# Row factors of the third block ahead of the second's, four row loads at later stages, and a fourth buffer in one temporary pool

## The chip, the cores and the metric

The kernel runs on one core of a Trainium2 chip. The metric is the device time of one execution in microseconds (us); three executions of the kernel before took 1470.12, 1470.48 and 1474.75 us, so its median is 1470.48 us.

## The reference

One layer of a decoder trunk for 4096 prompt tokens and 64 sample tokens (8 sequences of 8), 1024 wide:

```python
def _rmsnorm(x, g):
    xf = x.astype(jnp.float32)
    r = lax.rsqrt(jnp.mean(xf * xf, axis=-1, keepdims=True) + RMS_EPS)
    return (xf * r).astype(x.dtype) * g
...
    h = _rmsnorm(x, g_pre)
    z = h @ w_in
    cb, cc, ch, cg, q, k, v, ag, mq, mg = _split_cols(z)
...
    y = jnp.concatenate([out_a, out_b, out_c], axis=-1) @ w_out
    return x + _rmsnorm(y, g_post), new_conv, new_k, new_v
```

`out_a` is a gated short convolution, `out_b` sliding-window attention with a sink logit, `out_c` attention to 256 memory tokens, each times a gate. The outputs are the new activations and the key, value and convolution caches. The change is in the first part: the row factors `r` of the norm, and the projection `z`.

## The kernel before

The projection `h @ w_in` is done in three phases, each for some of the columns of `w_in` and for all 4160 tokens in 8 blocks of 520. TensorE keeps weights and activations as sums of two parts, named `hi` and `lo` (the rounded value, cast by ScalarE, and the rest, subtracted by VectorE at L361), so that a product takes three matmuls for each piece. A block is done by Strassen's scheme in 7 products; only the first two blocks of phase one (`PLAIN_BLOCKS`) are done as 8 plain products each, called stages (0,0) to (1,7) here. `plain_jobs` (L629) and `plain_loads` (L660) are tables by stage: which jobs for VectorE, ScalarE and GpSimd, and which loads, are issued while TensorE does that stage's product. After the projection come the attention and the output projection. TensorE's instruction order doesn't depend on the tables.

**The row factors.** The tokens are read in natural order in 40 groups of 104 rows (`nat`, 416 KB each), numbered `nat0`, `nat1`, ... in the order of their loads; five groups make a block. `row_step` (L269) squares one group on ScalarE with a running sum (L278); after the fifth group GpSimd turns the sums to factors `r` (L284, L285). For blocks 0 and 2 VectorE puts the factors on diagonals (`rows_diag`, L297, tile `mix_s`), and TensorE sums these with a matrix of ones, which leaves the factors broadcast over the partitions (`rows_product`, L306, 4 matmuls). For the other blocks GpSimd writes the 520 factors to memory (`rowd`, L290), and SyncE (SP in the profile) reads them back broadcast to 128 partitions (`rb<-rowd`, L253, 260 KB). `row_queue` issues that read back when a counter (`row_spreads`, 4 for every block) has run down, one step for each stage. Block 1's factors are applied to its already computed `z` (L625); block 2's are applied to its activations (L337), which are first multiplied by the gain of the norm (L328).

**The loads.** All loads of `nat`, `x` (the transposed activations, `in_xt`) and `rb` are issued by SP, one after the other in program order. A load that has to wait for a buffer, or for data that another DMA writes, holds up what is issued after it. `x` of block 2 goes to buffers `x_2B` (two halves) and `place` (two halves, each in two pieces of 344 and 176 KB, L240).

**Phase three.** `finish_parts` (L402) takes a finished `z` (128x520): ScalarE casts it to `zh` (L411), VectorE forms the rest `kl_` (L413), and SP stores both to `qd`. `zh` and `kl_` lie in temporary buffers of two pools, `t2a` and `t2b` of 3 buffers each, which are taken in turn (`temp`, L171); a buffer is free for its next use when the store from it has landed.

VectorE, ScalarE, GpSimd, SP and TensorE all run in program order through the projection (`manual_schedule`).

Of the kernel before, what the change touches and what calls it, by code (L numbers as in the profile page):

```python
# [12 lines left out]
ALU = mybir.AluOpType  # L13
# [7 lines left out]
NS = 64  # L21
# [23 lines left out]
PLAIN_BLOCKS = 2  # L45
# [7 lines left out]
def hybrid_layer(ctx: ExitStack, tc: tile.TileContext, a: dict):  # L53
    nc = tc.nc
    TE, V, S, G, DMA = nc.tensor, nc.vector, nc.scalar, nc.gpsimd, nc.sync
# [7 lines left out]
    ident = const.tile([P, P], F32, name="ident")  # L63
# [6 lines left out]
    diag = const.tile([P, 2 * HW], F32, name="mix_s")  # L70
# [25 lines left out]
    own = ExitStack()  # L96
# [3 lines left out]
    def z_pool(where, name, w=2):  # L100
        return where.enter_context(tc.tile_pool(name=name, bufs=1))

    def open_phase(ph):
        nonlocal tp, natp, pa2, pa1, wide
        wide = 0 if ph == 0 else 2

        if ph == 0:
            z = [z_pool(kept_z, f"z{n}") for n in range(4)]
            natp = own.enter_context(tc.tile_pool(name="nat", bufs=2))
            zp[2] = [*z, z_pool(own, "z4")]  # L110
            kept_z.z4 = zp[2][-1]
        elif ph == 1:
            zp[2].remove(kept_z.z4)
            zp[2][:0] = [z_pool(own, f"z{n}") for n in (5, 6, 7)]
        else:

            z = [z_pool(own, n) for n in ("z8", "z9", "y0", "y1", "z10", "y2")]
            tp = [own.enter_context(tc.tile_pool(name=f"t2{n}", bufs=3)) for n in "ab"]
            zp[2], zp[1] = [z[0], z[1], z[4]], [z[2], z[3], z[5]]
        if ph < 2:  # L120
            tp = own.enter_context(tc.tile_pool(name=f"t{ph}", bufs=(7, 9)[ph]))
        if ph != 1:

            psa.close()
            bank = lambda name, bufs: psa.enter_context(tc.tile_pool(name=name, bufs=bufs, space=bass.MemoryType.PSUM))
            if ph == 0:

                pa2 = {tag: bank(f"pa{tag}", 2) for tag in "xy"}
            else:

                pa1 = {(tag, w): bank(f"p{tag}{w}", 1) for tag, w in (("x", 2), ("x", 1), ("y", 1), ("y", 2))}
                third["ps"] = bank("psm", 2)

    tp = natp = pa2 = pa1 = wide = None

    def accumulator(i, w, name):

        tag = "xy"[i % 2]
        if pa1 is None:
            return pa2[tag].tile([P, 2, 512], F32, tag=tag, name=name)  # L140
        return pa1[tag, w].tile([P, w, 512], F32, tag="c", name=name)
# [28 lines left out]
    def temp(name, which=None):  # L170
        if isinstance(tp, list):  # L171
            third["turn"] = 1 - third.get("turn", 0)
            return tp[third["turn"] if which is None else which].tile([P, 2 * HW], F32, tag="t", name=name)
        return tp.tile([P, wide + 2 * HW], F32, tag="t", name=name)
# [69 lines left out]
    RG = 104  # L244

    rows = {}
    nat, sq, after_nat = {}, [0], [14]

    row_loads, row_spreads = [], {}

    def rows_load(b, again=False):
        rows[b] = (temp(f"rb{b}")[:, : 2 * HW] if again else natp.tile([P, 2 * HW], F32, tag="rb", name=f"rb{b}"))
        DMA.dma_start(rows[b], rowd[b].partition_broadcast(P))  # L253

    def row_load(j):
        if j < 5 * NBLK:
            g = RG * j - NS
            if 2 <= j < 10 or 12 <= j < 14:
                t = (wa if j < 7 or j == 12 else wb).tile([P, 2, 512], F32, tag="w", name=f"nat{j}")
                t = nat[j] = t.rearrange("p a n -> p (a n)")  # L260
            else:
                t = nat[j] = natp.tile([P, D], F32, tag="nat", name=f"nat{j}")
            if g < 0:
                DMA.dma_start(t[:NS], a["x_s"])
                DMA.dma_start(t[NS:RG], a["x_p"][: RG - NS, :])
            else:
                DMA.dma_start(t[:RG], a["x_p"][g : g + RG, :])

    def row_step():  # L269

        j = sq[0]
        if j == 5 * NBLK:
            return
        b, i = divmod(j, 5)
        if i == 0:
            nat["r"] = tiny.tile([P, 8], F32, tag="r", name=f"r{b}", bufs=3)
        r, t = nat["r"], nat.pop(j)
        S.activation(t[:RG], t[:RG], AF.Square, accum_out=r[:RG, i : i + 1])  # L278
        if j in (10, 11) or j >= 14:
            row_loads.append(after_nat[0])  # L280
            after_nat[0] += 1
        sq[0] += 1
        if i == 4:
            G.tensor_scalar(r[:RG, 0:5], r[:RG, 0:5], 1.0 / D, EPS, op0=ALU.mult, op1=ALU.add)  # L284
            G.tensor_tensor(r[:RG, 0:5], r[:RG, 0:5], mhalf[:RG, 0:5], op=ALU.pow)  # L285
            if b in (0, PLAIN_BLOCKS):
                nat["factors"] = r
            if b == PLAIN_BLOCKS:
                return
            G.dma_start(rowd[b].rearrange("(i p) -> p i", p=RG), r[:RG, 0:5])  # L290
            if b > 0:
                row_spreads[b] = 4

    def rows_diag():

        for i in range(5):
            V.tensor_scalar(diag[:RG, RG * i : RG * (i + 1)], ident[:RG, :RG], nat["factors"][:RG, i : i + 1], None, op0=ALU.mult)  # L297

    def rows_bank(b):
        rows[b] = accumulator(1, 2, f"rows_y{b}")[:, :, :HW]  # L300
# [327 lines left out]
    def plain_jobs(b, s):  # L628

        gains = lambda b, *os: [lambda o=o: x_gain(0, b, o) for o in os]  # L630
        scales = lambda b, *os: [lambda o=o: x_scale(0, b, o) for o in os]
        parts = lambda b, o: [lambda: x_split(b, o)]
        fill = lambda o: [lambda q=q: first_fill(o, q) for q in range(4)]
        sums = lambda q, k: [lambda: first_sums(q, k)]
        fills = lambda q, *os: [lambda o=o: first_fills(q, o) for o in os]
        done = lambda b, row: finish(0, b, zz[b], row)
        row = [row_step]
        return {
            (0, 0): lambda: [*fill("A11"), *parts(0, "B21")],
            (0, 1): lambda: fill("A22"),  # L640
            (0, 2): lambda: [*fill("A12"), *parts(0, "B12"), *row],
            (0, 3): lambda: [*sums(0, 0), *row, *sums(0, 1), *fills(0, "S2"), *row],
            (0, 4): lambda: [*parts(0, "B22"), *fills(0, "S3", "S1"), *row, *fills(0, "S4"), *row],
            (0, 5): lambda: [*sums(1, 0), *row, *sums(1, 1), *fills(1, "S2", "S3"), *row],
            (0, 6): lambda: [*parts(1, "B11"), *row, *fills(1, "S1", "S4"), *sums(3, 0), *row],
            (0, 7): lambda: [*row, *fills(3, "S2", "S3"), lambda: rows_diag()],
            (1, 0): lambda: [*parts(1, "B21"), *row, *row, lambda: rows_bank(0), lambda: rows_product(0), *z_rows(0, 1)],
            (1, 1): lambda: [*z_rows(0, 0), *done(0, 1), *row, *row],
            (1, 2): lambda: [*parts(1, "B12"), *done(0, 0), *fills(3, "S1"), *row],
            (1, 3): lambda: sums(2, 0),  # L650
            (1, 4): lambda: [*row, lambda: rows_diag(), lambda: rows_bank(2), *parts(1, "B22"), *gains(2, "B11"), *sums(2, 1),
                             *fills(2, "S2")],
            (1, 5): lambda: [lambda: rows_product(2), *fills(2, "S3"), *row, *fills(2, "S1"), *gains(2, "B21"), *fills(2, "S4"),
                             *row],
            (1, 6): lambda: [*scales(2, "B11"), *gains(2, "B12"), *scales(2, "B21", "B12"), *row],
            (1, 7): lambda: [lambda: h_split(0), *gains(2, "B22"), *scales(2, "B22"), lambda: t_sum(0, 2, "T1"), *row,
                             *z_rows(1, 1)],
        }[b, s]()

    def plain_loads(b, s):  # L660
        if s + b == 0:
            first_w("A22")
        for j in {(0, 0): (0,), (0, 1): (1,), (0, 2): (2, 3, 4), (0, 3): (5, 6, 7), (0, 4): (8, 9, 10), (0, 5): (11,),
                  (0, 7): (12, 13)}.get((b, s), ()):
            row_load(j)
        if (b, s) == (0, 1):
            first_w("A12")
        for nb, o in {(0, 1): [(0, "B12")], (0, 2): [(0, "B22")], (0, 3): [(1, "B11")], (0, 4): [(1, "B21")],
                      (0, 6): [(1, "B12")], (0, 7): [(1, "B22")], (1, 2): [(2, "B11")], (1, 3): [(2, "B21")],
                      (1, 4): [(2, "B12")], (1, 5): [(2, "B22")]}.get((b, s), ()):  # L670
            x_of(0, nb, o)
        row_queue()
# [1583 lines left out]
```

## Time and profile before

| | us |
|---|---|
| median of 3 executions | 1470.48 |
| the profiled execution | 1470.74 |
| its span, first to last instruction | 1469.0 |
| TensorE (PE) busy | 1453.3 (99%) |
| VectorE (DVE) busy | 1235.0 (84%) |
| ScalarE (ACT) busy | 888.9 (61%) |
| GpSimd (POOL) busy | 431.9 (29%) |
| mean granted TensorE clock | 0.999 of full |

The profiled execution is 1.74 us longer than its span, and 0.26 us above the median. In a row of the timeline the first number is the start in us from the span's beginning, the second the time in us, then engine, line, operation, output and inputs, the number of instructions in the row, and in brackets how long the engine had been idle before it and what ended that wait. PE is a matmul, PEld the load of its weights. SPq is SP's queue: its rows are issues of DMAs, not their transfers.

### The profile page before, as it was taken

Reading aid. Unit: us, or ns where it says so; the run is one execution under the profiler, and the core shown is the slowest. Engines: PE = TensorE matmul, PEld = TensorE weight load, DVE = VectorE, ACT = ScalarE, POOL = GpSimd, SP = SyncE. Lnnn points to the kernel's source line nnn. Section 1 sums busy time; section 2 is a strip of 40 time slices with the busy share of each in tenths; the row PEclk is TensorE's granted clock in tenths of the full one; section 3 lists DMA queues with packets and bytes.
Section 4 is the critical chain, followed back from the end, with each engine's and each line's share of the span. In section 5 each row is a group of like instructions: output and inputs, shape, how many; then the busy total and the mean of one; then the engine's idle time right before and its main releaser. Section 6 shows DMA issues by size and latency. Waiting matters only on the chain.

```text
span 1469.0 us, 31997 instructions
## 1 busy us (share of the span) xinstructions
PE 1453.3 (99%) x11887; PEld 1342.3 (91%) x11887; DVE 1235.0 (84%) x1991; ACT 888.9 (61%) x2170; POOL 431.9 (29%) x544
## 2 busy tenths in 40 slices
PE   9999999999999999999999999999999999999997
PEld 9999999999999999999999999778888888888875
DVE  6779887899988888798677777899998999999975
ACT  6776565566532222244545444788888878888862
POOL 0222322312403474300021130234334333433452
PEclk9999999999999999999999999999999999999999
DMA  9999999887866676688897679997887788888876
GB/s 265 191 248 223 297 275 265 248 288 248 216 229 244 243 248 232 225 284 253 281 233 266 215 215 329 279 280 240 252 263 241 240 243 268 243 248 264 254 266 224
DMA packets 233744, 369.59 MB, mean 252 GB/s; under 512 B 38501, under 2 KB 144485, under 8 KB 233557
## 3 DMA queue, kind: packets, MB, share of 16 engines
q1 hardware_dynamic: 210549, 314.66, 69.4%
q0 software_dynamic: 22320, 51.84, 12.4%
q8 instruction: 94, 1.54, 0.5%
q10 hardware_dynamic: 720, 1.05, 0.2%
q14 instruction: 61, 0.50, 0.1%
HBM read 251.00 MB, written 117.46 MB: 251 GB/s over the span
## 4 chain that ended last, share of the span: by engine, by line
PE 89%; DVE 4%; DMA 3%; ACT 2%; issue 1%; POOL 0%; ACTq 0%; SPq 0%; DVEq 0%; POOLq 0%
PE c L370 54%; PE y_c L1701 20%; PE ws L1394 3%; PE wo L1508 2%; PE wo L1115 2%; PE xs L1441 2%; PE wo L1503 1%; PE wt L1461 1%; PE xt L1461 1%; PE mem_acc L797 1%; DMA md<-th 1%; DMA nat<-in_x_p 1%; DMA ws4A<-in_w_in 1%; PE y L2069 1%; DMA md<-cacc 0%
## 5 line engine op out<-in xcount | busy, mean ns | idle before, releaser
L377 DVE TENSOR_TENSOR z<-c,z 128x520 f32<-128x520 f32 (+1 forms) x308 | 193.8, 643 | 71.8 <-PE c L370 70.8
L1425 ACT ACTIVATE sm<-sm,wnm 128x129 f32<-128x129 f32 x240 | 93.5, 392 | 13.8 <-DVE wrd L1429 7.1
L1701 PE MATMUL y_c<-wob,rows 128*128 128x512 f32 x384 | 95.8, 396 | 0.4 <-ACT s L1739 0.4
L1701 PE MATMUL y_c<-woT,a 128*128 128x512 f32 x384 | 95.2, 395 | 0.0
L1701 PE MATMUL y_c<-woT,down 128*128 128x512 f32 (+1 forms) x396 | 95.2, 389 | 0.0
L1701 PEld LDWEIGHTS y_c<-wob,rows 128*128 128x128 f32 x384 | 70.6, 188 | 17.5 <-ACT wpt L1366 2.4
L1701 PEld LDWEIGHTS y_c<-woT,down 128*128 128x128 f32 x396 | 71.7, 188 | 15.8 <-DVE swnm L1996 0.4
L1701 PEld LDWEIGHTS y_c<-woT,a 128*128 128x128 f32 x384 | 70.6, 188 | 15.2
L1232 ACT ACTIVATE xp<-xs,xnm 128x256 f32<-128x256 f32 x128 | 59.9, 483 | 20.4 <-PE wo L1115 13.5
L918 POOL TENSOR_TENSOR os0T<-os0T,os1T 128x512 f32<-128x512 f32 x20 | 29.0, 1448 | 125.2 <-DMA os1T<-in_w_out 75.8
L411 ACT CAST zh<-z 128x520 fp32r<-128x520 f32 x56 | 33.3, 625 | 40.9 <-DVE z L377 32.9
L1394 PEld LDWEIGHTS ws<-ring,q 128*128 128x128 f32 (+1 forms) x480 | 48.6, 186 | 8.4 <-issue 1.2
L278 ACT ACTIVATE nat<-nat 104x1024 f32<-104x1024 f32 x40 | 42.3, 1057 | 23.0 <-DMA nat<-in_x_p 23.0
L1411 DVE COPY_PREDICATED sm<-wmask,ws 128x512 f32<-128x512 uint8 x60 | 43.7, 754 | 14.6 <-ACT sm L1405 14.6
L1455 ACT ACTIVATE xp<-xp,xrd 128x256 f32<-128x256 f32 x120 | 53.9, 503 | 2.1 <-DVE xrd L1238 1.1
L1394 PE MATMUL ws<-ring,q 128*128 128x256 f32 (+1 forms) x480 | 54.0, 294 | 1.1 <-issue 0.6
L1366 ACT COPY wpt<-wt 128x512 f32<-128x512 f32 x60 | 33.9, 593 | 27.4 <-PE wo L1508 27.4
L379 ACT COPY z<-c 128x520 f32<-128x520 f32 (+1 forms) x44 | 24.2, 553 | 43.0 <-PE c L370 40.0
L1701 PE MATMUL y_c<-woT,diag 128*128 128x512 f32 x192 | 48.8, 400 | 0.0
L1369 POOL TENSOR_SCALAR_AFFINE_SELECT wpt<-wpt 128x512 f32<-128x512 f32 x64 | 46.1, 740 | 7.0 <-ACT wpt L1368 6.9
L1641 POOL TENSOR_TENSOR yst<-yst,mhalf 128x1 f32<-128x1 f32 (+1 forms) x33 | 20.4, 617 | 93.7 <-DVE yst L1640 93.7
L166 POOL DMA_DIRECT2D md<-th x48 | 26.2, 547 | 67.6 <-DVE th L430 59.4
(1055 smaller groups left out, 5537.9 us busy)
## 6 DMA issues: line engine op xcount, KB each, us to landing
woT<-tdT SPq DMA_DIRECT2D x75, 512.0 KB
q<-qd SPq DMA_DIRECT2D x112, 192.0 KB
xr<-in_x_p SPq DMA_DIRECT2D x32, 512.0 KB
nat<-in_x_p SPq DMA_DIRECT2D x39, 416.0 KB
o_yp<-xr SPq DMA_DIRECT2D x31, 512.0 KB
md<-th POOLq DMA_DIRECT2D x48, 260.0 KB, 7.2
qd<-zh SPq DMA_DIRECT2D x48, 260.0 KB
qd<-z SPq DMA_DIRECT2D x42, 260.0 KB
```

The lines of the kernel that those rows point to most:

```text
L278: S.activation(t[:RG], t[:RG], AF.Square, accum_out=r[:RG, i : i + 1])
L370: TE.matmul(bank[:, :HW], l, r, start=first and i == 0, stop=last and i == 3 * KH - 1)
L377: add = lambda dst, other: V.tensor_tensor(dst, c, other, op=ALU.add)
L411: S.copy(hi, z)
L1232: S.activation(p[:, i, :], s[:, i, :], AF.Exp, bias=nm[:, i : i + 1], scale=SCALE, accum_out=den[:, i : i + 1])
L1366: S.copy(p3.rearrange("p h (r q) -> p r h q", r=2), t)
L1369: select = lambda out, step, op, slope: lambda: G.affine_select(out, p3, pattern=[[0, 4], [step, P]], compare_op=op, fill=0.0, base=0, cha ...
L1394: TE.matmul(out(kvh, col, bank), q(kvh, col, bank)[r], k(kvh, part)[r], start=first, stop=True, skip_group_check=not first, **place)
L1411: V.copy_predicated(self.of[i].sms[kvh][:, :, :P].rearrange("p (h a) k -> p a h k", a=2), third["wmask"].unsqueeze(1).to_broadcast([P, 2, ...
L1425: S.activation(sm[:, hh, :], sm[:, hh, :], AF.Exp, bias=nm[:, hh : hh + 1], scale=SCALE, accum_out=den[:, hh : hh + 1])
L1455: S.mul(p[:, i, :], p[:, i, :], self.rds[h][:, i : i + 1])
L1701: TE.matmul(self.acc[bank], self.parts[name][:, l, j], wo[o][j][:, r, cs], start=new and j + i == 0, stop=j == 3 and i == 2, skip_group_ch ...
```

## The change

It has four parts.

1. Block 2's rows are loaded and squared ahead of block 1's (`row_block` swaps the two). `nat5` to `nat9` are now block 2's groups and `nat10` to `nat14` block 1's. The diagonals of block 2 are formed in stage (1,2) in place of (1,4). The write of block 1's factors now follows the second group of five, and the counter for reading them back is 2 for block 1 in place of 4.
2. Loads of row groups: `nat9` and `nat10` are issued in stage (0,5) in place of (0,4), and `nat11` in (0,6) in place of (0,5).
3. Pool `t2b` of phase three has 4 buffers in place of 3.
4. Through these the order of instructions moves at a few further places, below.

```diff
-            tp = [own.enter_context(tc.tile_pool(name=f"t2{n}", bufs=3)) for n in "ab"]
+            tp = [own.enter_context(tc.tile_pool(name=f"t2{n}", bufs=3 + (n == "b"))) for n in "ab"]
...
+    def row_block(n):
+
+        return {1: 2, 2: 1}.get(n, n)
+
...
-            g = RG * j - NS
+            g = RG * (5 * row_block(j // 5) + j % 5) - NS
...
-        b, i = divmod(j, 5)
+        b, i = row_block(j // 5), j % 5
...
-                nat["factors"] = r
+                nat["factors", b] = r
...
-                row_spreads[b] = 4
-
-    def rows_diag():
+                row_spreads[b] = 2 if b < PLAIN_BLOCKS else 4
+
+    def rows_diag(b):
...
-            (0, 7): lambda: [*row, *fills(3, "S2", "S3"), lambda: rows_diag()],
+            (0, 7): lambda: [*row, *fills(3, "S2", "S3"), lambda: rows_diag(0)],
...
-            (1, 2): lambda: [*parts(1, "B12"), *done(0, 0), *fills(3, "S1"), *row],
+            (1, 2): lambda: [*parts(1, "B12"), *done(0, 0), *fills(3, "S1"), *row, lambda: rows_diag(2)],
...
-            (1, 4): lambda: [*row, lambda: rows_diag(), lambda: rows_bank(2), *parts(1, "B22"), *gains(2, "B11"), *sums(2, 1),
+            (1, 4): lambda: [*row, lambda: rows_bank(2), *parts(1, "B22"), *gains(2, "B11"), *sums(2, 1),
...
-        for j in {(0, 0): (0,), (0, 1): (1,), (0, 2): (2, 3, 4), (0, 3): (5, 6, 7), (0, 4): (8, 9, 10), (0, 5): (11,),
+        for j in {(0, 0): (0,), (0, 1): (1,), (0, 2): (2, 3, 4), (0, 3): (5, 6, 7), (0, 4): (8,), (0, 5): (9, 10), (0, 6): (11,),
```

Lines of the changed file are 4 higher than before's from L254 on. TensorE's order is as before. Three places show what moves on the other engines.

On POOL, in stages (0,7) to (1,4), before: `rowd_76` is where block 1's factors are written, `r_700` holds them, `md<-th` and `qd<-kl_` are stores of block 0's results.

```order
L285 TENSOR_TENSOR r_700<-r_700,mhalf 104x5
L290 DMA rowd_76<-r_700 104x5x1
L166 DMA md<-th_3_989 128x520
L166 DMA md<-th_5_993 128x520
L166 DMA md<-th_7_1010 128x520
```

The same place on POOL after, from the first five groups' factors (now block 2's, `r_698`) on, and the rows where the write now stands.

```order
L289 TENSOR_TENSOR r_698<-r_698,mhalf 104x5
L166 DMA md<-th_3_988 128x520
...
L166 DMA qd<-zh_0_1094 128x520
L166 DMA qd<-kl__1096 128x520
L288 TENSOR_SCALAR r_922<-r_922 104x5
L289 TENSOR_TENSOR r_922<-r_922,mhalf 104x5
L294 DMA rowd_76<-r_922 104x5x1
L166 DMA hd_B_100<-x_2B_1030 128x1040
```

The write has moved behind ten stores and behind the second computation of factors.

On SP, in stages (1,4) to (1,6), before: `nat_1124` is `nat16`, `rb_1126` block 1's factors read back, `place` the second half of block 2's activations, `nat_1272` and `nat_1343` are `nat17` and `nat18`.

```order
L267 DMA nat_1124<-in_x_p 104x1024
L253 DMA rb_1126<-rowd_76 128x520
L240 DMA place<-in_xt 128x4x172
L240 DMA place<-in_xt 128x4x88
L240 DMA place<-in_xt 128x4x172
L240 DMA place<-in_xt 128x4x88
L267 DMA nat_1272<-in_x_p 104x1024
L267 DMA nat_1343<-in_x_p 104x1024
```

The same place on SP after (`nat_1129` is `nat16`).

```order
L271 DMA nat_1129<-in_x_p 104x1024
L240 DMA place<-in_xt 128x4x172
L240 DMA place<-in_xt 128x4x88
L257 DMA rb_1195<-rowd_76 128x520
L240 DMA place<-in_xt 128x4x172
L240 DMA place<-in_xt 128x4x88
L271 DMA nat_1272<-in_x_p 104x1024
L271 DMA nat_1343<-in_x_p 104x1024
```

The read back has moved behind the first half of `place`, and it still stands ahead of the second half and of `nat17`.

On VectorE in phase three, at the end of block 0 (`zh_2`, `zh_4`, `zh_6` are the last casts of block 0's `z`; `lo_1B` and `lo_1T` are parts that block 1's products read), before:

```order
L413 TENSOR_TENSOR kl__9072<-z_0_0_1_8683,zh_2_9070 128x520
L361 TENSOR_TENSOR lo_1B_9053<-x_1B_8937,hi_1B_9052 128x4x260
L413 TENSOR_TENSOR kl__9089<-z_0_0_1_8683,zh_4_9087 128x520
L361 TENSOR_TENSOR lo_1T_9127<-x_1T_8983,hi_1T_9126 128x4x260
L413 TENSOR_TENSOR kl__9093<-z_0_2_1_8710,zh_6_9091 128x520
```

The same place on VectorE after.

```order
L417 TENSOR_TENSOR kl__9072<-z_0_0_1_8683,zh_2_9070 128x520
L365 TENSOR_TENSOR lo_1B_9053<-x_1B_8937,hi_1B_9052 128x4x260
L417 TENSOR_TENSOR kl__9089<-z_0_0_1_8683,zh_4_9087 128x520
L417 TENSOR_TENSOR kl__9093<-z_0_2_1_8710,zh_6_9091 128x520
L365 TENSOR_TENSOR lo_1T_9127<-x_1T_8983,hi_1T_9126 128x4x260
```

`kl__9093` has moved ahead of `lo_1T`. With four buffers in `t2b`, `zh_2` waits for no store any more; `kl__9072` waits for the store of `kl__9004` (`kl__9021` before), `kl__9089` for that of `kl__9039`, `zh_6` for that of `zh_2`, and `kl__9093` for that of `kl__9072`. The five diagonals of block 2 on VectorE (L297) stand ahead of the weight sums of L603 to L611 in place of behind them, and the load of a small constant, `scol<-in_sinkcol`, which takes over memory that the temporaries held, stands later on SP: behind `gpost<-in_gpost` and ahead of a load of `woT` (L938), at the end of the projection.

More of the change, by code (lines that the diff above doesn't have):

```diff
@@ L291, in row_step @@
             if b > 0:
-                row_spreads[b] = 4
-    def rows_diag():
+                row_spreads[b] = 2 if b < PLAIN_BLOCKS else 4
+    def rows_diag(b):
         for i in range(5):
-            V.tensor_scalar(diag[:RG, RG * i : RG * (i + 1)], ident[:RG, :RG], nat["factors"][:RG, i : i + 1], None, op0=ALU.mult)
+            V.tensor_scalar(diag[:RG, RG * i : RG * (i + 1)], ident[:RG, :RG], nat["factors", b][:RG, i : i + 1], None, op0=ALU.mult)
     def rows_bank(b):
```

## Prediction

> **What bounds the kernel now.** I read the page's busy times first, then the stretches of time, then what TensorE (PE) waited for.
>
> ```profile
> span 1469.0 us, 31997 instructions
> PE 1453.3 (99%) x11887; PEld 1342.3 (91%) x11887; DVE 1235.0 (84%) x1991; ACT 888.9 (61%) x2170; POOL 431.9 (29%) x544
> ```
>
> PE is busy all but 15.7 us of the span. The stretches show how little of that lies where the change is: columns are the stretch, its length, then busy time of PE, PEld, DVE, ACT and POOL, the granted clock, the DMA share and GB/s.
>
> ```profile
> 6.00:100.00 94.00, 94.00 (x774) 93.43 (x775) 67.71 (x118) 70.47 (x142) 14.80 (x21) 1.00 0.97 237
> 100.00:112.00 12.00, 12.00 (x101) 11.81 (x100) 12.00 (x12) 8.04 (x14) 5.72 (x8) 1.00 0.87 202
> 690.00:700.00 10.00, 9.04 (x76) 8.83 (x76) 5.93 (x8) 5.00 (x9) 0.00 (x0) 1.00 0.82 293
> ```
>
> PE never waits from 6 to 112 us, where most of the edits are, and loses 0.96 us from 690 to 700, where phase three's first block ends. PE's own list of waits names the second.
>
> ```profile
> PE idle L707 <- POOL ident masks.py:199: 1.6, 1, 1.6
> PE c L370 <- DVE lo_1B L361: 1.0, 1, 1.0
> PE c L370 <- DVE lo_2T L361: 0.2, 1, 0.2
> ```
>
> So PE is the bound. The change leaves PE's work and order alone, so it can gain only waits (1.2 us in the last two rows; the first row is at the start, out of its reach), while any new wait of PE is lost in full. About 0.3%, 4.4 us, is what a measurement of this kernel can tell from no change.
>
> **Phase three: one more buffer.** These are the rows around PE's wait, by engine.
>
> ```profile
> 694.28 0.63 ACT L411 CAST zh<-z 128x520 fp32r<-128x520 f32 x1 [3.75 <-DMA qd<-kl__9004]
> 695.69 0.70 DVE L413 TENSOR_TENSOR kl__9072<-z,zh 128x520 fp32r<-128x520 f32 x1 [2.85 <-DMA qd<-kl__9021]
> 696.31 1.24 DVE L361 TENSOR_TENSOR lo_1B<-x_1B,hi_1B 128x1040 fp32r<-128x1040 f32 x1
> 696.36 0.28 PE L370 MATMUL c<-hi_1B,w_0A 128*128 128x260 f32 x1
> 697.60 0.39 PE L370 MATMUL c<-lo_1B,w_0A 128*128 128x260 f32 x1 [0.96 <-DVE lo_1B L361]
> ...
> 696.42 0.32 SPq L168 DMA_DIRECT2D qd<-kl__9072  x1
> 697.91 0.70 DVE L413 TENSOR_TENSOR kl__9089<-z,zh 128x520 fp32r<-128x520 f32 x1 [0.37 <-DMA qd<-zh]
> 702.12 0.70 DVE L413 TENSOR_TENSOR kl__9093<-z,zh 128x520 fp32r<-128x520 f32 x1 [1.46 <-DMA qd<-zh]
> 701.86 0.19 PEld L370 LDWEIGHTS c<-lo_1T,w_0S 128*128 128x128 f32 x1
> ```
>
> `kl__9072` waits for the store of `kl__9021` and holds up `lo_1B` behind it. With four buffers it waits for that of `kl__9004`, which had landed when ACT's row began, at 694.28. Then it starts 1.4 us earlier and `lo_1B` ends by 694.28 + 0.70 + 1.24 = 696.2, before PE wants it at 696.48 (0.12 behind the matmul at 696.36). The whole wait goes: 697.60 - 696.48 = 1.1 us.
>
> What is late next is `lo_1T`. It now stands behind `kl__9093`, which waits for the store of `kl__9072`. That store is issued at about 695.0. Two stores here bound its flight: `zh`'s, waited for by the row at 697.91, and the one waited for at 702.12; from their neighbours I estimate 3 to 5 us. So it lands at 698.0 to 700.0, `kl__9093` ends 0.70 later and `lo_1T` 1.24 after that, at 699.9 to 701.9; PE wants it at 701.86 - 1.1 = 700.8. It gives back 0 to 1.1, by the middle 0.2. Net: 0.9 gained, with 0 and 1.1 as ends.
>
> **Block 1's factors: write and read back.** The write on POOL now follows the second factors, and on SP the read back `rb` waits for it with half of `place`, `nat17` and all later loads queued behind it.
>
> ```profile
> 54.23 0.99 POOL L290 DMA_DIRECT2D rowd<-r  x1 [0.31 <-POOL r L285]
> 78.36 1.19 POOL L285 TENSOR_TENSOR r<-r,mhalf 104x5 f32<-104x5 f32 x1
> ...
> DMA to landing us min/median/max: 9.3/11.8/14.5
> ...
> 78.23 0.34 SPq L253 DMA_DIRECT2D rb<-rowd  x1
> 78.67 3.41 SPq L240 DMA_DIRECT2D place<-in_xt  x4
> 82.19 2.76 SPq L267 DMA_DIRECT2D nat<-in_x_p  x1
> ...
> 91.43 1.06 ACT L278 ACTIVATE nat<-nat 104x1024 f32<-104x1024 f32 x1 [1.90 <-DMA nat<-in_x_p]
> 97.62 0.60 ACT L688 COPY z<-c 128x520 f32<-128x520 f32 x1 [0.26 <-PE c L370]
> 98.11 1.72 ACT L328 ACTIVATE place<-place,gpre 128x260 f32<-128x260 f32 x4
> 99.86 1.24 DVE L337 TENSOR_TENSOR place<-place,rb 128x1040 f32<-128x1040 f32 x1 [1.22 <-ACT place L328]
> 110.92 1.23 DVE L361 TENSOR_TENSOR lo_2T<-x_2T,hi_2T 128x1040 fp32r<-128x1040 f32 x1
> 112.21 0.39 PE L370 MATMUL c<-lo_2T,w_0S 128*128 128x260 f32 x1 [0.18 <-DVE lo_2T L361]
> ```
>
> The row of landings is that of the seven `rowd` writes, from issue to landing. The write can be issued 0.3 us after the row at 78.36 ends: at 79.9. It can be earlier, since before's own write at 54.23 seems to slow the loads.
>
> ```profile
> 62.00:66.00 4.00, 4.00 (x35) 4.00 (x35) 3.40 (x5) 1.51 (x3) 1.45 (x3) 1.00 1.12 63
> 74.00:78.00 4.00, 4.00 (x36) 4.00 (x35) 2.65 (x4) 3.56 (x7) 2.38 (x5) 1.00 0.94 334
> ...
> 68.29 1.06 ACT L278 ACTIVATE nat<-nat 104x1024 f32<-104x1024 f32 x1 [4.77 <-DMA nat<-in_x_p]
> ```
>
> The DMA engines are full in both stretches and move 63 GB/s while the write is in flight, 334 later; ACT then waits 4.77 us for a row group. With the write gone from there, ACT's later rows can come up to some 3 us earlier (an estimate, bounded by the 4.77), and the write is issued between 76.9 and 79.9. I take 77.5, near the early end, since the wait is most of the delay. With the median flight of 11.8 it lands at 89.3; the ends are 76.9 + 9.3 = 86.2 and 79.9 + 14.5 = 94.4.
>
> Then come `rb`, half of `place` and `nat17`, 260 + 520 + 416 KB, 1.22 MB: 3.7 us at 334 GB/s, and I add 1 us for three issues of 0.3 to 0.4 ahead of `nat17`'s. `nat17` lands at 94.0 (89.9 to 100.1), 2.6 us behind the 91.4 at which ACT takes it now. From there the rows run without a hole: ACT idles 0.26 up to 97.62, ACT's gain of `place` ends as DVE's row at 99.86 begins, DVE is busy 12.00 of 12 us from 100 to 112, and its `lo_2T` is what PE waits for. So PE loses the delay less 0.26: 2.3 us, from 0 to 8.4. PE's stall isn't made up, since it idles nowhere else by as much.
>
> By the Trainium skill, "DMA: Bandwidth & Descriptors" (section "Anatomy of one DMA"), a DMA from GpSimd takes about 2.0 us plus its bytes over 436 GB/s, which for 2 KB of factors would be 2.0 us; by that the read back would hardly wait and the loss would be zero. This trace differs: 9.3 us is the shortest of seven, so the sum goes by the rows.
>
> **The early loads.** `nat9`, `nat10` and `nat11` are issued behind two pieces of `place`.
>
> ```profile
> 31.74 3.69 SPq L267 DMA_DIRECT2D nat<-in_x_p  x3
> 50.24 1.05 ACT L278 ACTIVATE nat<-nat 104x1024 f32<-104x1024 f32 x1
> 52.95 1.23 ACT L184 CAST w_3S<-wa3A 128x512 fp32r<-128x512 f32 x2 [1.10 <-DVE wa3A L610]
> ```
>
> The last of the three issues moves by some 3.6 us, to about 39; `nat9` is squared at 50.24, 11 us on, and ACT has 1.10 us to spare behind that. I cost it at nothing; without that cover it would be a us or two. Diagonals that come earlier gain nothing, since PE doesn't wait for `rows_y`.
>
> **The late constant.** `scol` now waits for stores of block 7, with a `woT` load behind it.
>
> ```profile
> 936.12 0.58 SPq L938 DMA_DIRECT2D woT<-tdT  x1
> 939.33 0.55 SPq L936 DMA_DIRECT2D woT<-trT  x1
> 946.07 0.50 PE L1701 MATMUL y_c<-woT,a 128*128 128x512 f32 x1
> ```
>
> The last store that it waits for stands ahead of the row at 936.12, so it is issued by 935.5; at 5 us of flight, as in phase three, this `woT` of 512 KB is issued at 940.5 and has 5.5 us until PE's product, where 512 KB take 1.8 us at the 293 GB/s of the stretch from 690. Nothing lost; 1 to 3 us if either flight is that much longer.
>
> **The sum.** 1470.74 for the profiled execution, less 0.9, plus 2.3: 1472.1. That execution lies 0.26 above the median, so the median should come to 1471.9.
>
> **The rivals.**
>
> *The read back costs nothing.* If the write lands by 87, `nat17` is there by 91.7 and only phase three's 0.9 is left: 1469.6. For it speaks the spread of flights (9.3 is one of seven) and that the earlier loads run free; against it the median of 11.8. The 2.0 us of the Trainium skill's page "DMA: Bandwidth & Descriptors" would lead here too, and the seven flights speak against it. Chance 0.27.
>
> *The read back costs its full price; slower.* With the write at 79.9 and a flight of 12.4 or more, it lands behind 92.3 and `nat17` behind 97.0: PE loses over 5.3 at 112, and the net is over 4.4. At 94.4 plus 4.7 the loss is 7.4 and the time 1470.5 - 0.9 + 7.4 = 1477.0. For it speaks that the longest flight, 14.5, is that of a write among heavy loads, as this one will be; against it that SP stands still meanwhile, so that the loads in the queues run out. Chance 0.17. By the Trainium skill, "TensorE: Matmul & The Clock Gate" (section "What's actually happening"), TensorE falls to half its clock after some 3.4 us of idleness and takes as long to return, which would add an estimated 1.7 us to such a stall. PE's wait of 0.96 left the clock at 1.00, and no stall here is long enough to show the rule.
>
> *`scol` holds the `woT` load beyond its 5.5 us*: some 2 us above the forecast, 1474. Chance 0.04.
>
> *Something faster that no row shows*, by over 4.4 us: the waits in reach are 1.2 us. Chance 0.02.
>
> **How the numbers follow.** The forecast case, a loss of up to 5.3 at 112 and a gain of 0 to 1.1 in phase three, has 0.50; its time runs from 1469.6 to 1474.9. Faster: 0.02. Slower by over 4.4 us: 0.17 and half of the `scol` case, 0.19. Within: 0.79. The range goes down to 1469.4, the gain alone at its end of 1.1, and up to 1476.6, inside the slower rival.
>
> **What would show it.** In the changed profile: no wait for `lo_1B` near 696 us, perhaps a short one for `lo_1T` near 701; the `rowd` write at 77 to 80 and `rb` on SP behind it at 87 to 94; low GB/s there and not at 62 to 66; ACT's wait for `nat17` longer than 1.90; PE waiting 2 to 3 us near 112 for `lo_2T`. The prediction is wrong if SP goes through `rb` by 85 or PE has no wait at 112, if PE waits for `rows_y` near 57 or 83, or if a wait appears at 946.

## The result, and the profile after

The changed kernel takes 1477.12 us (median of 7 executions, 1473.92 to 1479.11), the kernel before beside it 1470.87 (7 executions, 1470.12 to 1474.75). The ratio is 1.0033, with a 95% interval from 1.0019 to 1.0047: slower by 6.3 us by the medians, and by 4.9 us by the ratio, which is the figure that goes with the interval. The profiled execution took 1479.11 with a span of 1477.4, 8.4 above before's profiled one.

What PE waits for, by its list of waits after (total, times, longest):

```profile
PE c L374 <- ACT hi_2B L364: 4.6, 1, 4.6
PE rows_y L310 <- DVE mix_s L301: 1.8, 1, 1.8
PE c L374 <- DVE lo_2B L365: 0.7, 1, 0.7
```

Both old waits, for `lo_2T` in phase one and `lo_1B` in phase three, are gone; in their place stand one of 4.6 us at the start of block 2 and one of 1.8 at block 0's `rows_y`. The stretches of the same profile (length; busy PE, PEld, DVE, ACT, POOL; clock; DMA share; GB/s):

```profile
100.00:112.00 12.00, 6.67 (x39) 6.15 (x38) 5.34 (x5) 10.30 (x20) 1.69 (x4) 0.77 0.64 185
112.00:130.00 18.00, 18.00 (x148) 18.00 (x148) 17.76 (x21) 10.67 (x17) 7.63 (x11) 0.97 0.87 192
690.00:700.00 10.00, 10.00 (x87) 10.00 (x86) 9.28 (x14) 5.37 (x8) 0.00 (x0) 1.00 0.98 347
```

From 100 to 112, where before had 12.00 of 12 at a clock of 1.00, PE is busy 6.67 us and its clock is down to 0.77. From 690 to 700 it is busy throughout. Now the queue that was named in the prediction, and who takes `nat17` at its end (SP, POOL, ACT and PE of the profile after):

```profile
77.56 2.55 SPq L240 DMA_DIRECT2D place<-in_xt  x2
90.18 0.35 SPq L257 DMA_DIRECT2D rb<-rowd  x1
90.62 0.93 SPq L240 DMA_DIRECT2D place<-in_xt  x2
91.67 18.82 SPq L271 DMA_DIRECT2D nat<-in_x_p  x5
...
80.75 0.99 POOL L294 DMA_DIRECT2D rowd<-r  x1 [0.30 <-POOL r L289]
...
101.28 1.06 ACT L282 ACTIVATE nat<-nat 104x1024 f32<-104x1024 f32 x1 [9.81 <-DMA nat<-in_x_p]
...
107.06 0.59 PE L374 MATMUL c<-hi_2B,w_0A 128*128 128x260 f32 x1 [4.65 <-ACT hi_2B L364]
123.38 0.28 PE L374 MATMUL c<-hi_2T,w_1S 128*128 128x260 f32 x1
```

SP issues `place` until 80.1 and then nothing for 10 us, until the write issued at 80.75 has landed. `nat17`, issued at 91.67, is there at 101.28, where ACT has waited 9.81 us for it. The matmul at 123.38 is the same one that starts at 113.62 in before: 9.8 us later. The DMA engines in the meantime:

```profile
82.00:86.00 4.00, 4.00 (x34) 3.97 (x33) 2.82 (x6) 2.02 (x5) 0.00 (x0) 1.00 0.38 87
86.00:90.00 4.00, 4.00 (x33) 3.91 (x33) 1.32 (x2) 3.33 (x7) 0.00 (x0) 1.00 0.00 0
90.00:94.00 4.00, 4.00 (x35) 4.00 (x35) 2.57 (x4) 1.47 (x4) 0.12 (x1) 1.00 0.67 45
94.00:98.00 4.00, 4.00 (x36) 4.00 (x35) 0.50 (x1) 0.00 (x0) 0.99 (x2) 1.00 1.06 282
```

From 86 to 90, while SP waits, the records show no transfer at all, and from 90 to 94, behind `rb`, 45 GB/s. From 94 to 98 it is 282.

Phase three after, on VectorE:

```profile
703.25 0.70 DVE L417 TENSOR_TENSOR kl__9072<-z,zh 128x520 fp32r<-128x520 f32 x1 [1.22 <-DMA qd<-kl__9004]
703.87 1.24 DVE L365 TENSOR_TENSOR lo_1B<-x_1B,hi_1B 128x1040 fp32r<-128x1040 f32 x1
707.53 0.70 DVE L417 TENSOR_TENSOR kl__9093<-z,zh 128x520 fp32r<-128x520 f32 x1 [0.79 <-ACT zh L415]
708.71 1.24 DVE L365 TENSOR_TENSOR lo_1T<-x_1T,hi_1T 128x1040 fp32r<-128x1040 f32 x1 [0.47 <-PE c L374]
```

`kl__9072` waits for the store of `kl__9004` and `lo_1B` follows at once. From 694.93 to 699.01 in before's time, PE's lag behind before falls by 1.2 to 1.3 us.

### The profile page after: what moved, and what is told of

Same layout as the page of the kernel before. It is cut to its first block, busy times and chain, and to the rows that moved or that the text cites. A ratio compares the mean times of both kernels' runs of the same rounds, so it can differ in the third digit from the quotient of the medians.

```text
span 1477.4 us, 31993 instructions
## 1 busy us (share of the span) xinstructions
PE 1455.4 (99%) x11887; PEld 1344.7 (91%) x11887; DVE 1235.3 (84%) x1991; ACT 889.0 (60%) x2170; POOL 434.4 (29%) x544
## 3 DMA queue, kind: packets, MB, share of 16 engines
q0 software_dynamic: 22320, 51.84, 12.4%
## 4 chain that ended last, share of the span: by engine, by line
PE 88%; DMA 6%; DVE 2%; ACT 2%; SPq 1%; issue 1%; POOL 0%; ACTq 0%; DVEq 0%; POOLq 0%
PE c L374 54%; PE y_c L1705 20%; PE ws L1398 3%; DMA nat<-in_x_p 3%; PE wo L1512 2%; PE wo L1119 2%; PE xs L1445 2%; PE wt L1465 1%; PE wo L1507 1%; PE xt L1465 1%; PE mem_acc L801 1%; DMA rowd<-r 1%; DMA skm<-in_cmk 1%; DMA wr_0A<-in_w_in 1%; PE y L2073 1%
```

## The experiments

The theory after the result: block 1's read back, which waits on SP for the late write, is nearly the whole loss; the early loads cost about 2 us at `rows_y`; the half clock behind the stall costs about 3; the buffer gives 1.2 back. The rivals are given with each run. Ratios are to the kernel before beside it, with 95% intervals. On these chips before's own executions spread over some 10 us (1469.3 to 1479.7), so intervals are 0.1 to 0.2% wide to each side, and only effects over about 2 us show in them; smaller ones are read from PE's lag in the profiles (the start of the same matmul less its start in before's first profile). A profile shows one execution of each kernel.

**The kernel before, with the fourth buffer alone** (run twice, the second time beside other kernels).

```diff
-            tp = [own.enter_context(tc.tile_pool(name=f"t2{n}", bufs=3)) for n in "ab"]
+            tp = [own.enter_context(tc.tile_pool(name=f"t2{n}", bufs=3 + (n == "b"))) for n in "ab"]
```

> The kernel before with the fourth buffer of t2b alone. Theory: PE's wait of 1.0 for lo_1B near 696 us goes and no new one for lo_1T takes its place, since the changed kernel's profile shows PE 1.3 us nearer to before's times behind that place; time 1.0 to 1.3 under before, and nothing else moves by over 0.3 us. Rival: the gain in the changed kernel came from its being 9 us late there, with the transfers in another phase; then the wait for lo_1B goes but lo_1T, behind kl__9093, gives 0.5 or more of it back.

> The kernel before with the fourth buffer alone, once more, on this chip beside the others. Theory: PE's wait for lo_1B near 696 is gone in the profile, and the median is 0.5 to 1.3 under before, which five rounds may not tell apart from none. Rival: it is given back in phase three or later, and the last of PE's products stands where it stood in before's profile on such a chip.

Ratios 0.9996 (0.9984 to 1.0009) and 0.9992 (0.9980 to 1.0004). In both profiles PE is busy 10.00 of 10 us from 690 to 700, and its lag falls there by 1.2 and 1.3 us; in the second, 0.4 of it comes back at the first `lo_1T`. The gain is in the profile, and too small for the medians, which are 1.5 us above before's the first time and 0.3 under it the second. It isn't a sequel of the lag, since it is the same in the changed kernel, 8 us later, and here. Both profiles also have a wait for block 2's `rows_y` near 86, of 0.8 and 1.2 us, which neither profile of before has, and both are already 1.6 and 1.3 us behind at 40, after waits in the first 10 us. Up to phase three this kernel is before's, so waits like these can be a part of before's own spread.

**The kernel before, with the later loads alone.**

```diff
-(0, 4): (8, 9, 10), (0, 5): (11,),
+(0, 4): (8,), (0, 5): (9, 10), (0, 6): (11,),
```

> The kernel before with the later loads of nat9, nat10 and nat11 alone. Theory: nat9 lands near 54.7, ACT waits some 4.5 us for it ahead of the cast of w_3S, VectorE's diagonals come at 58 in place of 54.8 and PE waits 1.8 us for rows_y at 57; no half clock, since the wait is short; time 1.5 to 2.0 above before. Rival: nat9's wait came from something else in the changed kernel (the group it reads is another), and here the loads have the cover that was forecast: time within 0.3 of before, PE busy 4.00 of 4 us from 54 to 58.

Ratio 1.0002 (0.9989 to 1.0014). The profile, ACT and PE:

```profile
54.21 1.06 ACT L278 ACTIVATE nat<-nat 104x1024 f32<-104x1024 f32 x1 [5.08 <-DMA nat<-in_x_p]
...
58.63 1.12 PE L306 MATMUL rows_y<-mix_s,ones 104*128 104x260 f32 x4 [1.34 <-ACT hi_1B L589]
```

The wait is there, and PE is 1.6 us behind before's first profile at this place. The median is 1.9 above that of before, but the ratio is 0.3 us and its interval holds zero: the wait is shown, its price isn't.

**The changed order of row groups alone**, with the early loads and three buffers as before.

```diff
-            tp = [own.enter_context(tc.tile_pool(name=f"t2{n}", bufs=3 + (n == "b"))) for n in "ab"]
+            tp = [own.enter_context(tc.tile_pool(name=f"t2{n}", bufs=3)) for n in "ab"]
...
-(0, 4): (8,), (0, 5): (9, 10), (0, 6): (11,),
+(0, 4): (8, 9, 10), (0, 5): (11,),
```

> The changed order of the row groups alone: early loads and three buffers as before. Theory: rb on SP starts when the write of block 1's factors has landed, near 88 to 90, nat17 lands some 10 us behind that, PE waits 5 to 7 us near 100 for hi_2B and then runs at half clock for 4 to 6 us, which costs another 2 to 3.5; time 7 to 10 above before. Rival: the stall is a sequel of the late early loads (ACT 3 us late from 57 on); then it is gone here or under 2 us, and the clock stays at 1.00: time within 2 of before.

Ratio 1.0043 (1.0029 to 1.0057): a loss as large as the changed kernel's, without the late loads. SP and ACT:

```profile
86.33 0.34 SPq L257 DMA_DIRECT2D rb<-rowd  x1
...
96.06 1.06 ACT L282 ACTIVATE nat<-nat 104x1024 f32<-104x1024 f32 x1 [6.83 <-DMA nat<-in_x_p]
```

The rival is out. The wait of 5 to 7 us with a half clock behind it that the theory had didn't come, though: in the profiled execution the stall came in pieces of 1.7, 0.9 and 0.7 us, and the granted clock stayed at 1.00 in all stretches from 98 to 118, so this loss needs no half clock. It left PE 4.1 us behind at 120. Another 3.2 us came at 242 to 249, at waits of 0.6 and 0.9 us for `hi_5T` and `lo_5T` and 3.4 us of half clock behind them, so not all of this execution's loss is the read back's; whether the other executions have that second loss isn't shown.

**The changed kernel, read back later** (counter 4), and **one stage later** (counter 3; its edit is `row_spreads[b] = 3 if b < PLAIN_BLOCKS else 4`).

```diff
-                row_spreads[b] = 2 if b < PLAIN_BLOCKS else 4
+                row_spreads[b] = 4
```

> The changed kernel with the counter of block 1's read back at 4 in place of 2: on SP, rb now stands behind the rest of place, nat17, nat18 and nat19. Theory: SP doesn't stand still at 80 to 90, nat17 lands by 92, PE has no wait near 100 and the clock stays at 1.00; what is left is 1.9 at rows_y less 1.3 in phase three less 0.5 for lo_2T: time within 0.7 of before. Rival: the write itself slows all transfers after 81, wherever the read back stands; then nat17 is still 3 us or more late and the time is 3 or more above before.

> The changed kernel with block 1's counter at 3: rb stands behind the whole of place and nat17 and ahead of nat18 and nat19. Theory: nat17 lands by 92 to 96 as with the counter at 4; SP stands at rb until the write has landed near 88 to 91, and nat18 lands 5 to 6 us behind that, since the first 3 to 4 us behind rb move almost nothing; ACT wants nat18 at 95 to 99, so PE loses 0 to 2 and the clock stays at 1.00: time 0 to 3 above before. Rival: what delays nat17 in the changed kernel is the stores and loads around it and not rb; then nat18 lands within 3 us of rb's issue and nothing is lost: time as with the counter at 4.

Ratios 0.9997 (0.9983 to 1.0012) and 1.0003 (0.9992 to 1.0014): the loss is gone in both. The rival has a part, though. SP of the profile with counter 4, and ACT of the same:

```profile
83.00 14.47 SPq L271 DMA_DIRECT2D nat<-in_x_p  x3
97.59 0.83 SPq L257 DMA_DIRECT2D rb<-rowd  x1
...
95.98 1.06 ACT L282 ACTIVATE nat<-nat 104x1024 f32<-104x1024 f32 x1 [1.82 <-DMA nat<-in_x_p]
```

`nat17`, issued at 83.00 without waiting for anything, takes 13 us while the write is in flight; in before it took 9.2 (82.19 to 91.43). In this execution PE was already 4.6 us behind, for a wait of 2.5 us at `rows_y` and 3.4 us of half clock behind it, so `nat17` at 95.98 cost nothing more. It is one of the longest of the twelve (1478.31, median 1472.48), so it doesn't tell when `nat17` lands in the others; that the loss is gone is shown by the times. With counter 3 `nat17` came at 92.55 and PE was 0.6 us behind at the `hi_2T` product; `nat18`, issued behind `rb`, was in time at 96.21.

**The changed kernel with nothing to wait for**: block 1's read back fetches block 0's factors.

```diff
-        DMA.dma_start(rows[b], rowd[b].partition_broadcast(P))
+        DMA.dma_start(rows[b], rowd[0 if b == 1 and not again else b].partition_broadcast(P))
```

> The changed kernel, but block 1's read back fetches the factors of block 0, which were written long before: the same load at the same place of SP's queue with nothing to wait for. The results of block 1 are computed with the wrong factors; all else is as in the changed kernel. Theory: the wait for the write is the whole of the loss at 100: SP issues rb near 80, nat17 lands by 93, PE has no wait at 100 and no half clock there; time as with the late read back, within 1.5 of before. Rival: the load rb itself (260 KB out of 2 KB, 45 GB/s in the stretch where it flies) delays what is behind it by some 3 us; then nat17 comes at 94 or later, PE loses 1 to 3 near 100 to 112, and the time is 2 to 4 above before.

Ratio 0.9999 (0.9989 to 1.0009). SP:

```profile
79.40 1.02 SPq L240 DMA_DIRECT2D place<-in_xt  x2
80.51 2.19 SPq L257 DMA_DIRECT2D rb<-rowd  x1
82.79 0.94 SPq L240 DMA_DIRECT2D place<-in_xt  x2
```

The same load at the same place, without the wait, costs nothing that shows in the times: the wait is the loss. The profile is less clear. It is the longest of the twelve executions (1474.67), PE waited 2.6 us for `rows_y` and was 4.7 us behind by 66; `nat17` was taken at 96.37, which is the rival's sign, and PE had no wait near 100 because it was late itself.

**The changed kernel, unchanged, and the kernel before, unchanged**, beside these.

> The changed kernel, unchanged, on this chip, so that it stands beside the experiments. Theory: as in its first profile, SP waits at rb until the write has landed near 90, PE waits 5 us or more near 102 and then runs at half clock; 6 to 9 above before. Rival: the late early loads and the read back are each worth half; then the time is only 2 to 4 above before here, and the wait near 102 is under 3 us with the clock at 1.00.

> The kernel before, unchanged, profiled on this chip. The executions of before spread here from 1469.6 to 1479.7. Theory: the spread comes from PE waits on late loads in the first 115 us and near 240, whose landings differ from one execution to the next; then this profile has PE waits that the first one had not, by as much as its time is longer, and no half clock. Rival: the spread lies in the attention part, behind 930 us; then its first 900 us agree with the first profile within 1 us.

The changed kernel: 1.0034 (1.0023 to 1.0044), as before; the profiled execution was one of the fastest, 1474.01. It has no wait at `rows_y` at all, `rb` at 88.02, and `nat17` taken at 97.64. The rival's short waits near 102 were there (1.6 and 0.9), but with the half clock that the rival left out. The medians are 6.1 us apart, as in the theory; the ratio's 5.0 lies between the two. The kernel before: ratio 1.0000; its profile (1469.95) has a wait of 0.6 for `lo_1B` in place of 1.0 and agrees with the first within 0.9 us all through. It was one of the shortest executions, so it doesn't tell where before's spread comes from.

**The changed kernel, the write from SP** in place of POOL, right ahead of the read back.

```diff
-            G.dma_start(rowd[b].rearrange("(i p) -> p i", p=RG), r[:RG, 0:5])
+            if b == 1:
+                nat["factors", b] = r
+            else:
+                G.dma_start(rowd[b].rearrange("(i p) -> p i", p=RG), r[:RG, 0:5])
...
+        if b == 1 and not again:
+            DMA.dma_start(rowd[b].rearrange("(i p) -> p i", p=RG), nat["factors", b][:RG, 0:5])
         DMA.dma_start(rows[b], rowd[b].partition_broadcast(P))
```

> The changed kernel with the write of block 1's factors issued by SP, right ahead of the read back, in place of POOL. It tells whose the 9 us from issue to landing are. Theory: they are of the path through POOL, since the DMA engines' records are empty for the last 5 to 6 of them; then the write lands in 2 to 4 us from SP, rb is issued near 84, nat17 lands by 95 and PE loses under 2 near 100; time within 2.5 of before. Rival: they are of the write itself, 520 pieces of 4 bytes, from whatever queue; then rb is issued at 89 or later and the time is as the changed kernel's, 6 above before.

Ratio 1.0033 (1.0019 to 1.0047). SP:

```profile
81.26 0.35 SPq L258 DMA_DIRECT2D rowd<-r  x1
90.36 0.34 SPq L259 DMA_DIRECT2D rb<-rowd  x1
```

9.1 us from SP, 9.4 from POOL (80.75 to 90.18): my expectation was wrong and the rival right. The flight belongs to this write, 520 pieces of 4 bytes, and not to the queue that issues it. That the small pieces make it long wasn't tried.

**The changed kernel with 24 matmuls in the stall.**

```diff
+                if (ph, b, p, q) == (0, PLAIN_BLOCKS, 0, 0):
+                    fill = ws[ph, q, PRODUCTS[p][0]]
+                    for _ in range(24):
+                        TE.matmul(acc[:, 0, :HW], fill[:, 0, :P], fill[:, 0, :HW], start=True, stop=True)
                 product(ws[ph, q, PRODUCTS[p][0]], hs[i], acc[:, q % 2])
```

> The changed kernel with 24 more matmuls on PE (2.9 us) at the place of the stall, into the accumulator that block 2's first product clears; they need nothing that is late, so PE runs them while it would stand idle, and the results are as before. Theory: PE's idle time there falls from 4 to 5 us to 2 or less, the granted clock stays at 1.00 and the 2.5 to 3 us of half clock go, while the filler itself is hidden: 2 to 3 under the changed kernel, 3 to 4 above before. Rival: the half clock isn't the price (the matmuls behind the stall are late because their operands are); then the time is the changed kernel's, or above it by part of the 2.9.

Ratio 1.0044 (1.0024 to 1.0065): no gain over the changed kernel. First the stretches of the changed kernel's second profile, then of this one:

```profile
104.00:106.00 2.00, 1.31 (x7) 1.31 (x8) 1.13 (x2) 2.00 (x5) 0.00 (x0) 0.74 0.78 226
106.00:108.00 2.00, 2.00 (x11) 2.00 (x11) 2.00 (x3) 1.95 (x4) 0.83 (x2) 0.50 0.92 232
```

```profile
104.00:106.00 2.00, 1.11 (x8) 0.71 (x6) 1.08 (x1) 2.00 (x4) 0.51 (x1) 1.00 0.63 70
106.00:108.00 2.00, 1.78 (x15) 1.78 (x16) 1.13 (x2) 2.00 (x6) 0.00 (x0) 1.00 0.83 268
112.00:114.00 2.00, 1.27 (x11) 1.06 (x10) 2.00 (x3) 0.84 (x2) 0.91 (x1) 1.00 0.99 332
```

The filler does what it should: the clock stays at 1.00. The time that PE saves it then waits for `lo_2B`: at 106 for the subtraction on VectorE, which had itself waited for ScalarE's cast of `hi_2B` (ScalarE is busy 2.00 of 2 us there), and at 113 for VectorE, which is now busy 2.00 of 2 us. So the half clock is real and costs next to nothing here. The theory's 3 us for it is out.

**What fits all of them.** The prediction's chain from `nat17` to PE can be measured in each profile: ACT takes `nat17`, and PE comes to the second part of the `hi_2T` product (the row at 113.62 in before). PE's lag at 96, ahead of the place, and at that row tells whether PE lost time in between.

```profile
113.62 0.28 PE L370 MATMUL c<-hi_2T,w_1S 128*128 128x260 f32 x1
```

| profile | ACT takes `nat17` | PE at `hi_2T`, `w_1S` | between | PE's lag at 96, at that row |
|---|---|---|---|---|
| before | 91.43 | 113.62 | 22.2 | 0, 0 |
| after, first profile | 101.28 | 123.38 | 22.1 | 1.9, 9.8 |
| after, second profile | 97.64 | 119.26 | 21.6 | 1.3, 5.6 |
| row order alone | 96.06 | 117.69 | 21.6 | -0.3, 4.1 |
| read back at 3 | 92.55 | 114.21 | 21.7 | 0.0, 0.6 |
| write from SP | 100.15 | 121.77 | 21.6 | 1.7, 8.1 |
| filler | 99.16 | 120.79 | 21.6 | 1.4, 7.2 |
| read back at 4 | 95.98 | 118.27 | 22.3 | 4.6, 4.7 |
| block 0's factors | 96.37 | 118.29 | 21.9 | 4.7, 4.7 |

In the six profiles in which PE lost time here, the distance is 21.6 to 22.1 over arrivals from 92.55 to 101.28, with the half clock (after, write from SP) and without (filler, row order), with the wait at `rows_y` (after's first) and without (its second). In these PE's lag at this place is `nat17`'s delay less 0.1 to 0.6 us, and the smaller lags ahead of it don't add to it. In the last two rows PE lost nothing here, since it was as late as `nat17` already, so they don't test the chain; nor do the five profiles that the table leaves out, in which PE's lag doesn't change from 96 to 120 either and the distance is 22.1 to 24.2.

The half clock isn't always free. Behind the waits of 2.5 and 2.6 us for `rows_y` (read back at 4, block 0's factors) it lasted 3.4 us and PE's lag grew by 1.7 to 1.8 us beyond the wait. There PE had nothing else to wait for.

**The order of the row groups and the buffer, with the early loads and the counter at 4.** What is left of the change once its two losses are undone.

```diff
-                row_spreads[b] = 2 if b < PLAIN_BLOCKS else 4
+                row_spreads[b] = 4
...
-(0, 4): (8,), (0, 5): (9, 10), (0, 6): (11,),
+(0, 4): (8, 9, 10), (0, 5): (11,),
```

> The changed kernel with the read back's counter at 4 and the early loads as before: what is left is the order of the row groups and the fourth buffer. Theory: no wait of PE at 57 beyond 1.0, none near 100, none for lo_1B at 696; time 1 to 2 under before, the fastest of the kernels so far. Rival: the order itself costs where it was not looked for (POOL's write at 77 to 81 against the loads of block 2); then PE waits 1 us or more between 100 and 115 and the time is within 0.5 of before or above.

Ratio 0.9991 (0.9982 to 1.0000), median 1469.66 beside 1471.40. In its profile `nat17` is taken at 89.77 without a wait, PE doesn't wait for `rows_y`, its lag stays under 1.2 us up to phase three, and falls there by 1.2. It is the fastest of the kernels, at the edge of what can be told from before; against the buffer alone (0.9992) it shows nothing, so no time is shown for the order of the groups by itself.

## Why the forecast was too low

**The place and the mechanism were right.** SP stood at `rb` until the write had landed, `nat17` came late, ACT and VectorE passed that on without a hole, and PE lost the delay less 0.26: 101.28 - 91.43 - 0.26 = 9.6, where 9.8 was measured at 113.62. That is the slower rival (1477.0), which had a chance of 0.17, and not the forecast (1471.9). By the ratio the time is 1475.3 on the scale of the prediction, inside its range up to 1476.6; but the forecast case ended at 1474.9, so the range held the time only because it reached into the rival.

**The step that failed** is the term "`nat17` 4.7 us behind the write's landing", worked out as 1.22 MB at 334 GB/s and three issues. It measured 11.1 us (90.18 to 101.28), and 9.6 in the second profile (88.02 to 97.64); 101.28 is later even than the 100.1 that I had as the late end. I had divided by the best rate of the trace and left out the flight of `nat17`, which stood in the rows that I showed: issued at 82.19, waited for by ACT until 91.43, so 9.2 us from issue to landing. After, the same flight took 9.6 us (91.67 to 101.28) and 8.1 in the second profile (89.50 to 97.64), much as in before. The write's landing at 89.3, 1.5 us for the issues and 9.2 us would have made 100.0, a loss of 8.3 us, and 1477.9. So a load that stands behind the wait comes a whole flight after its issue, and not after its share of the bandwidth. What fills that flight is open: the 45 GB/s of the stretch from 90 to 94, `nat18` behind it on SP, and POOL's two stores of 520 KB at 93.89 and 95.02 may each have a part, and none was tried by itself.

**The write's landing** came out well by luck: 89.3 forecast, 90.18 measured, with two misses that nearly cancel (issued 3.3 us later than the 77.5 that I took, flight 9.4 in place of 11.8). I also misread the row of landings: the trace has the landing of only four of the seven writes (14.5, 12.4, 11.2 and 9.3 us), so 9.3 is the shortest of four. Without the late loads the issue came at 77.28 (row order alone), so the early estimate was right for that case: ACT's wait for `nat9` pushes the write back.

**The early loads** were costed at nothing and made PE wait 1.8 us for `rows_y` in the first profile, 1.3 to 2.6 in three others with these loads, and none in four, the second profile of the changed kernel among them. `nat9` was issued at 36.60 in place of 33.55 and landed at 54.71, 18 us on, where I had counted 11 us as cover: again a load's flight was sized too short. ACT's 1.10 us to spare weren't enough for the 4.8 to 6.0 us that it waited. A wait for `rows_y` near 57 was one of the prediction's own signs of being wrong. In the changed kernel itself this wait is swallowed by the larger one.

**The wait at 112 for `lo_2T`** that I named as the place of the loss came at 102, for `hi_2B`: with a delay this long `hi_2B`, which was ready 2.9 us ahead of PE in before (97.36 against 100.30), is late as well. The sum doesn't change by it, though no wait at 112 was one of the prediction's own signs of being wrong.

**The clock.** PE fell to 0.50 behind the wait of 4.6 us, and behind waits of 2.5 and 2.6 us at `rows_y` (read back at 4, block 0's factors), and stayed at 1.00 behind 1.8. Each time the half clock lasted 3.4 us, or twice that (6.8 us, after's first profile). The Trainium skill's page "TensorE: Matmul & The Clock Gate" (section "What's actually happening") has about 3.4 us of idleness as the time after which the clock halves; the trace agrees on the half clock, but shows it after 2.5 us, and with the row order alone after two waits of 0.6 and 0.9 us near 243. The prediction's 1.7 us for it were lost at `rows_y` in these two profiles; behind the stall at 102 they were lost on paper only, since PE waits for ScalarE and VectorE there anyway.

**Phase three** was right: the wait for `lo_1B` went in all ten profiles with the buffer, PE's lag falls there by 1.1 to 1.3 us, and 0.3 to 0.8 came back at `lo_1T` in four of them. `scol` held nothing up: PE's waits after don't name its `woT`.

What stays open is the price of the late loads by themselves (median 1.9, interval -1.6 to +2.1 us), and where the rest of before's own spread of executions comes from.

## What to carry to other kernels

A read back that waits for a late write is paid by everything behind it on its queue, so look for what stands behind the wait, and put the wait behind the loads that are due, as the counter of 4 does. Follow the late load along the in-order engines to the bound engine: if the chain has no hole, the loss is the delay, and smaller stalls of the bound engine ahead of it don't add to it. Half a clock is hidden too while the engine waits for others, and costs its full price where it doesn't. When you size a landing, take the time from issue to landing of a like load under like traffic, here the 9.2 us of the same load in before, rather than bytes over the best rate.

## What the hardware showed that was not expected

A write of 2 KB in 520 pieces of 4 bytes takes 9 us to land from either queue, 9.4 from POOL and 9.1 from SP, and other such writes in these profiles took 8.9 to 15.0. In the changed kernel's profile the DMA engines' records are empty from 86 to 90, the last four of the 9.4 us, and SP's next loads start only then. What is in flight with such a write is slow too: with the read back at 4, where SP didn't wait, a load of 416 KB took 13 us in place of 9.2, and these are the stretches of that profile (columns as above):

```profile
82.00:86.00 4.00, 4.00 (x36) 4.00 (x35) 2.56 (x6) 4.00 (x10) 0.06 (x1) 1.00 1.08 285
86.00:90.00 4.00, 4.00 (x32) 3.88 (x31) 1.13 (x2) 1.35 (x4) 0.00 (x0) 1.00 0.73 61
90.00:94.00 4.00, 4.00 (x36) 4.00 (x35) 1.39 (x2) 4.00 (x9) 0.00 (x0) 1.00 0.29 20
```

The stretch from 62 to 66, which moved 63 GB/s in before with the write of 54.23 in flight, moved 216 GB/s after, where that write is gone:

```profile
62.00:66.00 4.00, 4.00 (x36) 4.00 (x35) 3.93 (x4) 2.69 (x6) 0.00 (x0) 1.00 0.96 216
```
